# A hybrid decoder trunk on one core: normalisation rows applied through DRAM at the output projection's load

## Chip, cores and metric

The kernel runs on one core of a Trainium2 chip. The metric is the device time of one launch in microseconds; the time of a kernel is the median of its runs.

## What is computed

Two layers over 1024 positions of width 1024, all in float32. Each layer normalises its input, projects it once, and hands the pieces to three mixers that run side by side: a gated linear recurrence (512 channels in four blocks of 128), differential attention (four heads of 128) and a matrix-memory recurrence, "mLSTM" (four heads of 128). Their 1536 outputs go through one output projection; a convolutional gated MLP follows. Every mixer output is normalised by an RMS factor per position, and it is this step that the change touches:

```python
def rmsnorm(x, g):
    y = xf * lax.rsqrt(jnp.mean(xf * xf, axis=-1, keepdims=True) + EPS)
    return (y * g).astype(x.dtype)

y_rg = rmsnorm(gelu(gb) * h, norm_g)                 # over all 512 channels
o    = rmsnorm(o, norm_g) * (1.0 - lambda_init)      # attention, per head of 128
h    = rmsnorm(h, norm_g.reshape(H, dh)) * sigmoid(o_pre)   # mLSTM, per head of 128
x = x + concatenate([y_rg, y_da, y_ml], axis=-1) @ w_out[l]
```

## The kernel before, in words

Activations lie with channels on the 128 partitions and the 1024 positions along the free dimension. So the sum of squares over channels is a sum over partitions, and the factor of a position must come back to all partitions before it can multiply.

Every large product is done three times in a rounded format (`mm3`, L130: high times high, low times high, high times low), after `split` (L126) has cut a tile into its high part (ScalarE) and its low part (VectorE).

A mixer's RMS factors are made in three steps. `compact` (L244) takes the squares of a 128x1024 tile and multiplies them, 128 positions at a time, with a column of ones: eight matmuls with one output column, so that position 128i+p lands in row p and column i of a 128x8 tile. `rsqrt` (L222) turns the small tile into factors with some ten VectorE instructions. `bcast_half` (L235) brings the factors of 512 positions back: four matmuls, each with one column of the factors broadcast as the stationary operand and the identity as the moving one, into a PSUM tile of 128x512.

- `rg` (L467), the recurrence, runs once per block. It writes the unscaled output `u` to DRAM (L502), squares it on ScalarE (L503), compacts the squares (L246) and adds the result to `rgacc`, a 128x8 tile (L507, L509). After the fourth block the factors `rg_r` are made.
- `da_attn` (L634), attention, one head in two halves of queries (`A0` to `A7`). After the second half it squares `o`, compacts, makes the factors, multiplies `o` in place from the two PSUM tiles (L696) and stores it (L698).
- `ml_head` (L819), mLSTM, the same in two halves (`M0` to `M7`), with the scaling at L891 and the store at L894.
- `yload` (L1004) reads four of the twelve stored tiles back (L1009) and splits them into operands of the output projection. For the recurrence (`y0`) the factors are broadcast first, copied by ScalarE into an SBUF tile `rgb` (L996), and each tile is multiplied on load (L1011). For attention (`y1`) and mLSTM (`y2`) nothing is multiplied there.
- `w_out` (L896) multiplies four loaded tiles with four of the eight column blocks of the output weights (`w0` to `w5`), and adds the result to the residual.

The order of all this is a list of steps per layer written out by hand (`ORDER`, L32); `step` (L966) turns a step's name into a call. A scheduler of the framework sets the order on each engine from the program's order, a priority (`high_priority` for a few instructions) and a model of durations; every engine then works through its own queue strictly in order, and so do the DMA queues: SyncE (SP) issues nearly all DMAs, GpSimd (POOL) those that accumulate. A DMA whose tile is not yet free or whose source is not yet written holds back all DMAs behind it on its queue.

Tiles come from small rings, and a new one waits until the oldest is released: `mu` has 2 tiles of 128x1024 (used by the convolutions, the recurrence's operands, the value projection and `rgb`), `p4` 4 (the loaded tiles among others), `o4` 2 (`o`, `num`, the squares), `mr` 3 of 128x512 (the decay rows `R` and `E` of mLSTM), `x16` 2 of four rows each (the recurrence's work space, attention's probabilities, the residual), `h4` 16 (the operands of the projections), and PSUM `aux` 2 banks (compacts, broadcasts, transposes, sums). mLSTM's rows `R` (L851) are DMAs that broadcast one row of DRAM to 128 partitions; POOL masks them (L852) before ScalarE takes their exponential.

Of the kernel before, what the change touches and what calls it, by code (L numbers as in the profile page):

```python
# [32 lines left out]
    "v0 r s0 R0 q0 g q2 q3 q1 A0 z3 z1 v1 A1 z0 A2 R1 z2 A3 A4 A5 M0 M1 z6 A6 A7 z5 z4 z11 M2 z8 R2 M3 R3 z7 z9 z10 y1 M4 y0 M5 w3 M6 s1 w1 M7 w0 w2 y2 w5 w4".split(),  # L33
    "R0 q0 q1 g z0 v0 z7 v1 q3 A0 q2 A1 A2 z2 A3 A4 z1 z3 z5 A5 M0 z4 z6 M1 R1 A6 A7 M2 z8 R2 M3 R3 z11 M4 z9 z10 y1 M5 y0 M6 M7 w3 w2 w0 w1 y2 w4 w5".split(),
# [18 lines left out]
class Trunk:  # L53
# [181 lines left out]
    def bcast_half(self, r, j, ps):  # L235
        nc = self.nc
        pb = ps.tile([P, HALF], F32, tag="aux", name=self.nm("pbc"))
        for i in range(4):
            c = 4 * j + i
            nc.tensor.matmul(pb[:, i * P : (i + 1) * P], r[:, c : c + 1].broadcast_to([P, P]),  # L240
                             self.ident, start=True, stop=True)
        return pb

# [223 lines left out]
    def rg(self, l, n):  # L467
        nc, a, d = self.nc, self.a, self.lay[l]
        if n == 0:
            self.rgacc = self.sm("rgacc", (P, 8), bufs=1)  # L470
        for _ in (0,):
# [32 lines left out]
            pc = self.aux()  # L504
            self.compact(pc, i, self.ones_d)
            if n == 0:
                nc.vector.tensor_copy(self.rgacc, pc[:, :8])  # L507
            else:
                nc.vector.tensor_tensor(self.rgacc, self.rgacc, pc[:, :8], ALU.add)  # L509
        if n < 3:  # L510
            return
        v = self.sm("nv", (P, 8))
        nc.vector.tensor_scalar(v, self.rgacc, 2.0, EPS, ALU.mult, ALU.add)
        self.rg_r = self.sm("rgr", (P, 8), bufs=1)
        self.rsqrt(self.rg_r, v)
# [118 lines left out]
    def da_attn(self, l, h, g):  # L634
# [49 lines left out]
        if g == 0:  # L684
            return
        sq = self.o4("sq")
# [7 lines left out]
        for j in range(2):  # L694
            t = slice(j * HALF, (j + 1) * HALF)
            nc.vector.scalar_tensor_tensor(o[:, t], o[:, t], d["dn2"], self.bcast_half(r, j, self.ps), ALU.mult, ALU.mult)  # L696
        self.yd[4 + h] = self.dr("yd")
        nc.sync.dma_start(self.yd[4 + h], o)  # L698
# [120 lines left out]
    def ml_head(self, l, h, hf):  # L819
# [69 lines left out]
        for j in range(2):  # L889
            t = slice(j * HALF, (j + 1) * HALF)  # L890
            nc.vector.scalar_tensor_tensor(num[:, t], num[:, t], d["mn2"][:, h : h + 1],  # L891
                                           self.bcast_half(r, j, self.ps), ALU.mult, ALU.mult)
# [19 lines left out]
    def mixer(self, l):  # L912
        nc = self.nc
        with ExitStack() as c:
# [4 lines left out]
            self.yd = [None] * 12  # L919
# [46 lines left out]
    def step(self, l, step):  # L966
# [19 lines left out]
        elif k == "z":  # L986
            self.ml_z(l, n // 3, n % 3)
        elif k == "M":
            self.ml_head(l, n // 2, n % 2)
        elif k == "R":  # L990
            self.rg(l, n)
        elif k == "y":
            if n == 0:
                rb = self.mu("rgb")
                for j in range(2):
                    self.nc.scalar.copy(rb[:, j * HALF : (j + 1) * HALF], self.bcast_half(self.rg_r, j, self.ps))  # L996
                self.ys[n] = self.yload(range(4), rb, self.lay[l]["rn"])
            else:
                self.ys[n] = self.yload(range(4 * n, 4 * n + 4))
        elif k == "w":  # L1000
            ms = range(4 * (n % 2), 4 * (n % 2) + 4)
            self.w_out(l, 4 * (n // 2), self.ys[n // 2], self.x[ms[0]] is None, ms)

    def yload(self, ks, rb=None, g=None):  # L1004
        nc = self.nc
        ys = []
        for k in ks:
            st = self.p4("yst")
            nc.sync.dma_start(st, self.yd[k])  # L1009
            if g is not None:  # L1010
                nc.vector.scalar_tensor_tensor(st, st, g[:, k : k + 1], rb, ALU.mult, ALU.mult)  # L1011
            hi, lo = self.h4("yh"), self.h4("yl")
# [318 lines left out]
```

## Time and profile before

| | us |
|---|---|
| median of 3 runs | 2988.64 |
| lowest and highest run | 2980.81, 2997.79 |
| the profiled execution's own time | 3000.99 |
| span of its trace | 2999.3 |
| granted TensorE clock, mean over the span | 0.978 |

The profile is one execution. PE is TensorE's matmuls, PEld its weight loads, DVE VectorE, ACT ScalarE, POOL GpSimd, SP SyncE; a "q" marks a queue's issuing. Matmuls are pipelined, so that the time one costs is the distance between two starts and not its printed duration. A float32 matmul has two records, one in the rounded format has one. The granted clock is a share of full speed (2.4 GHz); 0.5 is the lower level of 1.2 GHz. The first layer's mixers fill about 60 to 770 us of the span, its MLP lasts to about 1505, the second layer's mixers to about 2225.

### The profile page before, as it was taken

The page shows a single profiled execution, that of the slowest core. Times are in us where ns is not written, and L with a number is a line of the kernel's source. Part 1 is how long each engine was busy: PE and PEld are TensorE (multiplying, and loading weights), DVE is VectorE, ACT ScalarE, POOL GpSimd, SP SyncE. Part 2 cuts the span into 40 slices and gives each one's busy share as a digit, 9 for nine tenths or more (in the row PEclk, how much of TensorE's full clock was granted, in tenths as well). Part 3 has the DMA queues.
Part 4 walks back from the last instruction along what each step waited for, and adds up shares of the span by engine and source line. Part 5 has one row for each costly group of instructions (what it writes and reads, how often), then busy time and mean ns, then how long its engine had stood idle before and what let it go on. Part 6 is the DMA issues. An engine that isn't in the chain of part 4 may idle for free.

```text
span 2999.3 us, 37078 instructions
## 1 busy us (share of the span) xinstructions
PE 2898.1 (97%) x13433; PEld 2363.2 (79%) x13433; DVE 2065.0 (69%) x3399; ACT 1346.3 (45%) x2160; POOL 280.5 (9%) x304
## 2 busy tenths in 40 slices
PE   8999999999999999999999999999998999999998
PEld 6777777877878888778877877787776788887887
DVE  5674787786698888844384378787756988887434
ACT  4423655653454444522252346566424544444223
POOL 1000002112111111000010000202111111110000
PEclk9999999998999999999999999999999999999999
DMA  5332224353455555543423322325543555556323
GB/s 188 84 98 95 79 68 123 91 201 112 123 116 127 127 127 127 162 142 95 142 74 102 98 85 92 94 78 161 162 115 99 116 127 123 127 127 211 103 71 110
DMA packets 403428, 352.57 MB, mean 118 GB/s; under 512 B 22226, under 2 KB 348684, under 8 KB 403244
## 3 DMA queue, kind: packets, MB, share of 16 engines
q1 hardware_dynamic: 355900, 326.33, 35.2%
q0 software_dynamic: 46464, 23.07, 6.3%
q8 instruction: 106, 1.74, 0.2%
q10 hardware_dynamic: 880, 0.79, 0.1%
q14 instruction: 78, 0.64, 0.1%
HBM read 263.61 MB, written 86.51 MB: 117 GB/s over the span
## 4 chain that ended last, share of the span: by engine, by line
PE 79%; DVE 8%; DMA 5%; ACT 3%; issue 2%; POOL 1%; SPq 0%; DVEq 0%; POOLq 0%; ACTq 0%
PE z L137 23%; PE z L136 23%; PE z L135 23%; DMA R<-Rd 2%; PE aux L246 2%; DMA fst<-fa 1%; PE pbc L240 1%; PE sc L655 1%; PE sc L656 1%; PE aux L135 1%; PE aux L671 1%; PE aux L136 1%; PE aux L137 1%; DVE wlo L128 1%; POOL ds L864 0%
## 5 line engine op out<-in xcount | busy, mean ns | idle before, releaser
L127 ACT CAST whi<-wraw 128x512 fp32r<-128x512 f32 (+1 forms) x416 | 254.4, 613 | 717.6 <-PE z L136 534.8
L128 DVE TENSOR_TENSOR wlo<-wraw,whi 128x512 fp32r<-128x512 f32 (+1 forms) x416 | 284.3, 684 | 150.1 <-ACT whi L127 146.7
L136 PE MATMUL z<-hl,whi 128*128 128x512 f32 x896 | 363.5, 406 | 4.7 <-DVE hl L265 4.7
L135 PE MATMUL z<-hh,whi 128*128 128x512 f32 x896 | 363.4, 406 | 0.9 <-DVE mpad L459 0.9
L137 PE MATMUL z<-hh,wlo 128*128 128x512 f32 x896 | 362.0, 404 | 0.0
L135 PE MATMUL z<-xh,whi 128*128 128x512 f32 x704 | 276.8, 394 | 5.3 <-ACT cv L1171 2.8
L136 PE MATMUL z<-xh,whi 128*128 128x512 f32 x704 | 276.2, 392 | 4.3 <-DVE xh L128 4.3
L135 PE MATMUL z<-ah,whi 128*128 128x512 f32 x704 | 271.9, 392 | 8.1 <-ACT ah L127 7.8
L137 PE MATMUL z<-xh,wlo 128*128 128x512 f32 x704 | 275.4, 391 | 0.0
L136 PE MATMUL z<-ah,whi 128*128 128x512 f32 x704 | 273.8, 390 | 0.2 <-DVE ah L128 0.2
L137 PE MATMUL z<-ah,wlo 128*128 128x512 f32 x704 | 273.5, 390 | 0.0
L1148 DVE SCALAR_TENSOR_TENSOR fc<-cv,fpar,fc 128x1024 f32<-128x1024 f32 x176 | 222.0, 1281 | 2.9 <-ACT fc L1145 0.6
L127 ACT CAST whi<-fraw 128x512 fp32r<-128x512 f32 x180 | 111.4, 619 | 246.4 <-PE z L136 239.9
L135 PE MATMUL z<-xu,whi 128*128 128x512 f32 x528 | 205.8, 390 | 0.3 <-ACT cv L1171 0.3
L136 PE MATMUL z<-xu,whi 128*128 128x512 f32 x528 | 205.5, 389 | 0.0
L137 PE MATMUL z<-xu,wlo 128*128 128x512 f32 x528 | 205.3, 389 | 0.0
L136 PEld LDWEIGHTS z<-hl,whi 128*128 128x128 f32 x896 | 172.8, 193 | 41.3 <-DVE hl L265 9.0
L135 PEld LDWEIGHTS z<-hh,whi 128*128 128x128 f32 x896 | 173.0, 193 | 34.0 <-DVE mpad L459 0.9
L137 PEld LDWEIGHTS z<-hh,wlo 128*128 128x128 f32 x896 | 173.0, 193 | 31.7
L1140 POOL DMA_DIRECT2D fraw<-in_w_up_dram x88 | 113.3, 1304 | 733.7 <-DVE cv L1171 343.8
L135 PEld LDWEIGHTS z<-ah,whi 128*128 128x128 f32 x704 | 131.5, 188 | 39.6 <-ACT ah L127 12.0
L135 PEld LDWEIGHTS z<-xh,whi 128*128 128x128 f32 x704 | 133.2, 189 | 35.1 <-ACT xh L127 4.1
(384 smaller groups left out, 6134.0 us busy)
## 6 DMA issues: line engine op xcount, KB each, us to landing
wraw<-in_w_up_dram SPq DMA_DIRECT2D x128, 256.0 KB
wraw<-in_w_in_dram SPq DMA_DIRECT2D x112, 256.0 KB
wraw<-in_w_down_dram SPq DMA_DIRECT2D x112, 256.0 KB
fraw<-in_w_up_dram SPq DMA_DIRECT2D x92, 256.0 KB
fraw<-in_w_up_dram POOLq DMA_DIRECT2D x88, 256.0 KB, 5.7
fa<-fc SPq DMA_DIRECT2D x44, 512.0 KB
xd<-x SPq DMA_DIRECT2D x32, 512.0 KB
x<-xd SPq DMA_DIRECT2D x32, 512.0 KB
```

The lines of the kernel that those rows point to most:

```text
L127: self.nc.scalar.copy(hi, src)
L128: self.nc.vector.tensor_tensor(lo, src, hi.bitcast(F32), ALU.subtract)
L135: nc.tensor.matmul(out, ah, bh, start=start and i == 0, stop=False, **kw)
L136: nc.tensor.matmul(out, ah, bl, start=False, stop=False, **kw)
L137: nc.tensor.matmul(out, al, bh, start=False, stop=stop and i == last, **kw)
L240: nc.tensor.matmul(pb[:, i * P : (i + 1) * P], r[:, c : c + 1].broadcast_to([P, P]), self.ident, start=True, stop=True)
L246: self.nc.tensor.matmul(pc[:, i : i + 1], sq[:, i * P : (i + 1) * P], ones, start=True, stop=True)
L655: nc.tensor.matmul(dst, qq[c][:, qs], k[:, :kn], start=True, stop=False)
L656: nc.tensor.matmul(dst, ql[c][:, qs], k[:, :kn], start=False, stop=kb < g)
L671: nc.tensor.transpose(pa[:, k * P : (k + 1) * P], pp[0][:, (4 * kb + k) * P : (4 * kb + k + 1) * P], self.ident)
L1140: nc.gpsimd.dma_start(t, rows(*more), accum_op=ALU.add)
L1148: nc.vector.scalar_tensor_tensor(o, u[:, j : j + S], cw[:, j, col : col + 1], o, ALU.mult, ALU.add)
```

## The change

Seven of a layer's eight head factors (four attention heads, mLSTM heads 0 to 2) and the recurrence's factor are no longer broadcast by matmuls. `row_out` transposes the 128x8 factors to 8x128, copies them out of PSUM and writes them to DRAM as one row of 1024; `row_in` loads such a row into a `mu` tile, broadcast to 128 partitions; `yload` multiplies there. mLSTM head 3 stays as it was. The recurrence's squares are written to a DRAM tile by the first block and added to it by accumulating DMAs of POOL for the other three; a new step `c` loads the sum, compacts it once and makes the factors.

```diff
+    (ORDER, first layer)  ... z7 z9 c z10 y1 M4 y0 ...
+    (ORDER, second layer) ... R3 z11 M4 c z9 z10 y1 M5 y0 ...
...
+    def row_out(self, r):
+        nc = self.nc
+        t = self.dr("rbd", (8, P))
+        pt = self.aux()
+        nc.tensor.transpose(pt[:8, :P], r, self.ident)
+        c = self.tp.tile([P, HALF], F32, tag="mr", bufs=3, name=self.nm("rt"))[:8, :P]
+        nc.scalar.copy(c, pt[:8, :P])
+        nc.sync.dma_start(t, c)
+        return t
+
+    def row_in(self, t, dst):
+        self.nc.sync.dma_start(dst, t.rearrange("i p -> (i p)").unsqueeze(0).broadcast_to([P, S]))
+        return dst
...
     def rg(self, l, n):
...
-            self.rgacc = self.sm("rgacc", (P, 8), bufs=1)
+            self.rgacc = self.dr("rgacc")
...
             nc.scalar.activation(i, u, AF.Square)
-            pc = self.aux()
-            self.compact(pc, i, self.ones_d)
-            if n == 0:
-                nc.vector.tensor_copy(self.rgacc, pc[:, :8])
-            else:
-                nc.vector.tensor_tensor(self.rgacc, self.rgacc, pc[:, :8], ALU.add)
-        if n < 3:
-            return
-        v = self.sm("nv", (P, 8))
-        nc.vector.tensor_scalar(v, self.rgacc, 2.0, EPS, ALU.mult, ALU.add)
-        self.rg_r = self.sm("rgr", (P, 8), bufs=1)
-        self.rsqrt(self.rg_r, v)
+            nc.gpsimd.dma_start(self.rgacc, i, **({"accum_op": ALU.add} if n else {}))
+
+    def rg_stats(self):
+        nc = self.nc
+        t5 = self.p4("rgs")
+        nc.sync.dma_start(t5, self.rgacc)
+        pc = self.aux()
+        self.compact(pc, t5, self.ones_d)
+        v, r = self.sm("nv", (P, 8)), self.sm("nr", (P, 8))
+        nc.vector.tensor_scalar(v, pc[:, :8], 2.0, EPS, ALU.mult, ALU.add)
+        self.rsqrt(r, v)
+        self.rg_r = self.row_out(r)
...
     (da_attn)
+        self.yd[4 + h] = self.dr("yd")
+        nc.sync.dma_start(self.yd[4 + h], o)
         sq = self.o4("sq")
...
         self.rsqrt(r, v)
-        for j in range(2):
-            t = slice(j * HALF, (j + 1) * HALF)
-            nc.vector.scalar_tensor_tensor(o[:, t], o[:, t], d["dn2"], self.bcast_half(r, j, self.ps), ALU.mult, ALU.mult)
-        self.yd[4 + h] = self.dr("yd")
-        nc.sync.dma_start(self.yd[4 + h], o)
+        self.yrow[4 + h] = self.row_out(r), d["dn2"]
...
     (ml_head)
-        for j in range(2):
-            t = slice(j * HALF, (j + 1) * HALF)
-            nc.vector.scalar_tensor_tensor(num[:, t], num[:, t], d["mn2"][:, h : h + 1],
-                                           self.bcast_half(r, j, self.ps), ALU.mult, ALU.mult)
+        if h < 3:
+            self.yrow[8 + h] = self.row_out(r), d["mn2"][:, h : h + 1]
+        else:
+            for j in range(2):
...
         self.yd[8 + h] = self.dr("yd")
         nc.sync.dma_start(self.yd[8 + h], num)
...
     (step)
             if n == 0:
-                rb = self.mu("rgb")
-                for j in range(2):
-                    self.nc.scalar.copy(rb[:, j * HALF : (j + 1) * HALF], self.bcast_half(self.rg_r, j, self.ps))
+                rb = self.row_in(self.rg_r, self.mu("rgb"))
...
+        elif k == "c":
+            self.rg_stats()
...
     (yload)
+            elif k in self.yrow:
+                row, w = self.yrow[k]
+                nc.vector.scalar_tensor_tensor(st, st, w, self.row_in(row, self.mu("yrb")), ALU.mult, ALU.mult)
```

## Rows read from the trace of the kernel before

**Rows 1.** The page: busy time by engine; the chain that ended last, by engine.

```profile
PE 2898.1 (97%) x13433; PEld 2363.2 (79%) x13433; DVE 2065.0 (69%) x3399; ACT 1346.3 (45%) x2160; POOL 280.5 (9%) x304
...
PE 79%; DVE 8%; DMA 5%; ACT 3%; issue 2%; POOL 1%; SPq 0%; DVEq 0%; POOLq 0%; ACTq 0%
```

**Rows 2.** Stretches: us; PE, PEld, DVE, ACT, POOL busy; clock; DMA share; GB/s.

```profile
600.00:635.00 35.00, 34.42 (x172) 28.77 (x171) 26.50 (x49) 19.44 (x21) 0.75 (x2) 0.95 0.61 213
635.00:680.00 45.00, 41.54 (x207) 33.55 (x206) 38.74 (x52) 24.70 (x38) 7.04 (x8) 1.00 0.52 170
```

**Rows 3.** Timeline of PE: start, duration; a broadcast, a compact, five transposes, and what follows.

```profile
609.39 1.95 PE L240 MATMUL pbc<-identr,nr 128*128 128x128 f32 x16
611.09 0.48 PE L137 MATMUL z<-hh,wlo 128*128 128x512 f32 x1
...
603.45 1.84 PE L246 MATMUL aux<-ones_h,sq 128*128 128x1 f32 x16
605.15 0.47 PE L136 MATMUL rgz<-ul,rgw 128*128 128x512 f32 x1
...
335.05 0.71 PE L671 MATMUL aux<-identr,p 128*128 128x128 f32 x5
335.52 0.47 PE L135 MATMUL z<-hh,whi 128*128 128x512 f32 x1
```

**Rows 4.** Groups by line: recurrence's compacts; busy, mean ns, idle before and its releaser.

```profile
L246 PE MATMUL aux<-ones_d,rg 128*128 128x1 f32 x128 | 17.0, 263 | 10.6 <-ACT rg L503 10.6
```

**Rows 5.** Stretches right behind six of the eight recurrence compacts, columns as in rows 2.

```profile
132.00:136.00 4.00, 4.00 (x12) 3.17 (x11) 3.42 (x7) 1.25 (x2) 0.00 (x0) 0.57 0.04 4
...
374.00:382.00 8.00, 8.00 (x32) 6.51 (x32) 3.59 (x8) 1.63 (x4) 0.00 (x0) 0.57 0.02 6
...
589.00:600.00 11.00, 11.00 (x40) 9.65 (x40) 4.90 (x10) 5.05 (x8) 2.12 (x3) 0.53 0.69 179
...
627.00:631.00 4.00, 4.00 (x12) 3.15 (x11) 2.41 (x10) 3.04 (x4) 0.00 (x0) 0.57 0.59 173
...
2053.00:2058.00 5.00, 5.00 (x24) 4.41 (x24) 3.42 (x7) 0.97 (x2) 1.06 (x2) 0.66 0.39 105
...
2088.00:2095.00 7.00, 7.00 (x26) 6.32 (x26) 3.15 (x16) 0.80 (x3) 0.57 (x2) 0.51 0.44 104
```

**Rows 6.** The scalings and small copies: duration min/median/max in ns, first and last start.

```profile
L696 DVE SCALAR_TENSOR_TENSOR o<-o,par,pbc x16: 737/748/750, 332.8 to 2020.3; 128x512 f32<-128x512 f32 x16
...
L1011 DVE SCALAR_TENSOR_TENSOR yst<-yst,par,rgb x8: 1272/1279/1285, 669.6 to 2167.6; 128x1024 f32<-128x1024 f32 x8
...
L871 ACT ACTIVATE mpc<-aux x16: 162/173/176, 471.7 to 2198.9; 128x4 f32<-128x4 f32 x16
```

**Rows 7.** SP's loads of the stored tiles, and ScalarE's splits of them.

```profile
L1009 SPq DMA_DIRECT2D yst<-yd x24: 319/320/596, 600.3 to 2218.7; - x24
L127 ACT CAST yh<-yst x24: 1030/1047/1052, 635.4 to 2222.0; 128x1024 fp32r<-128x1024 f32 x24
```

**Rows 8.** The chain in order of time: broadcast row loads; R3's compact, layer one.

```profile
683.36 3.40 DMA R<-Rd
...
717.34 5.35 DMA R<-Rd
...
624.64 1.95 PE aux L246 x16
```

**Rows 9.** Waits of SP's queue: us in total, times, longest.

```profile
SPq L111 <- DVE wlo L128: 714.8, 214, 16.3
...
SPq L894 <- DVE num L891: 24.4, 8, 6.4
```

**Rows 10.** The page: POOL's accumulating DMAs of the MLP, issue and landing.

```profile
L1140 POOL DMA_DIRECT2D fraw<-in_w_up_dram x88 | 113.3, 1304 | 733.7 <-DVE cv L1171 343.8
...
fraw<-in_w_up_dram POOLq DMA_DIRECT2D x88, 256.0 KB, 5.7
```

**Rows 11.** Matmuls that broadcast the recurrence's factors: duration in ns, first and last start.

```profile
L240 PE MATMUL pbc<-identr,rgr x32: 270/275/276, 666.7 to 2157.5; 128*128 128x128 f32 x32
```

More of the change, by code (lines that the diff above doesn't have):

```diff
@@ L32 @@
 ORDER = (
-    "v0 r s0 R0 q0 g q2 q3 q1 A0 z3 z1 v1 A1 z0 A2 R1 z2 A3 A4 A5 M0 M1 z6 A6 A7 z5 z4 z11 M2 z8 R2 M3 R3 z7 z9 z10 y1 M4 y0 M5 w3 M6 s1 w1 M7 w0 w2 y2 w5 w4".split(),
-    "R0 q0 q1 g z0 v0 z7 v1 q3 A0 q2 A1 A2 z2 A3 A4 z1 z3 z5 A5 M0 z4 z6 M1 R1 A6 A7 M2 z8 R2 M3 R3 z11 M4 z9 z10 y1 M5 y0 M6 M7 w3 w2 w0 w1 y2 w4 w5".split(),
+    "v0 r s0 R0 q0 g q2 q3 q1 A0 z3 z1 v1 A1 z0 A2 R1 z2 A3 A4 A5 M0 M1 z6 A6 A7 z5 z4 z11 M2 z8 R2 M3 R3 z7 z9 c z10 y1 M4 y0 M5 w3 M6 s1 w1 M7 w0 w2 y2 w5 w4".split(),
+    "R0 q0 q1 g z0 v0 z7 v1 q3 A0 q2 A1 A2 z2 A3 A4 z1 z3 z5 A5 M0 z4 z6 M1 R1 A6 A7 M2 z8 R2 M3 R3 z11 M4 c z9 z10 y1 M5 y0 M6 M7 w3 w2 w0 w1 y2 w4 w5".split(),
 )
@@ L888, in ml_head @@
         nc.vector.scalar_tensor_tensor(num, th, 1.0, num, ALU.add, ALU.mult)
-        for j in range(2):
-            t = slice(j * HALF, (j + 1) * HALF)
-            nc.vector.scalar_tensor_tensor(num[:, t], num[:, t], d["mn2"][:, h : h + 1],
-                                           self.bcast_half(r, j, self.ps), ALU.mult, ALU.mult)
+        if h < 3:
+            self.yrow[8 + h] = self.row_out(r), d["mn2"][:, h : h + 1]
+        else:
+            for j in range(2):
+                t = slice(j * HALF, (j + 1) * HALF)
+                nc.vector.scalar_tensor_tensor(num[:, t], num[:, t], d["mn2"][:, h : h + 1],
+                                               self.bcast_half(r, j, self.ps), ALU.mult, ALU.mult)
         self.yd[8 + h] = self.dr("yd")
@@ L918, in mixer @@
             self.tp = self.pool(c, "mt", 2)
-            self.yd = [None] * 12
+            self.yd, self.yrow = [None] * 12, {}
             self.pads = [self.tp.tile([P, S + 3], F32, tag=f"mpad{i}", bufs=1, name=self.nm("mpad"))
```

## The prediction

> **What bounds the kernel now.** I read the busy times and the chain of waits first [rows 1]. TensorE's matmuls are busy for 97% of the span and make up 79% of the chain that ended last; no other engine has more than 8% of it. So an instruction taken off TensorE is worth nearly its own time, unless it stood in a stretch where something else ends last. The stretches tell where that may be [rows 2]: ahead of the output projection TensorE is filled, 34.4 of 35 us; while the operands are loaded and split, VectorE has 38.7 of 45 us and TensorE only 41.5. There VectorE and transfers count too. What an instruction of TensorE costs I take from the distance between starts, since printed durations overlap [rows 3].
>
> **What leaves TensorE.** A row's broadcast is two calls, 16 records, from 609.39 to 611.09: 1.70 us [rows 3]. Per layer four attention heads, three mLSTM heads and the recurrence lose theirs: 16 rows x 1.70 = 27.2 us. A compact is 16 records from 603.45 to 605.15, also 1.70 us [rows 3]. The recurrence has 8 of them (128 records, [rows 4]) and keeps one a layer: 6 x 1.70 = 10.2 us. New are 16 transposes of 128x8. The nearest row is five transposes of 128x128 in 335.05 to 335.52, 0.094 us each [rows 3]: 1.5 us. Net 27.2 + 10.2 - 1.5 = 35.9 us. Since some of this lay beside VectorE's full stretches, I count nine tenths, **-32**; between 24 (only two thirds bound) and 36.
>
> **Waits and clock around the compacts.** TensorE stood idle 10.6 us in all before the eight recurrence compacts, each time for ScalarE's square [rows 4]: its queue is in order, and the compact came round before the squares were there. Six of eight go: 8 us; the remaining two wait for a DMA instead, so I take **-6**, between 0 and -10.6. Behind six of the eight compacts the granted clock fell to the level of 1.2 GHz: over the six stretches, length x (1 - clock) is 1.7 + 3.4 + 5.2 + 1.7 + 1.7 + 3.4 = 17.1 us of lost work [rows 5]. In the worst, TensorE had waited for the square and then done one-column matmuls, and the clock stood at 0.53 for 11 us. That is 2.1 us a compact, 12.8 for six. A wait elsewhere can take the clock down as well, so I take about half, **-7**, between 0 and -17.
>
> **VectorE.** Gone are 14 rows' scalings out of PSUM, 28 x 0.748 = 20.9 us (attention's row; mLSTM's have the same shape); new are 14 scalings at load, each like the one that the recurrence's tiles already have there, 14 x 1.279 = 17.9 us [rows 6]. In sum that is -3, but the work moves, out of the attention and mLSTM steps, where TensorE hides it, into the loads. There VectorE is 76% to 86% busy [rows 2]. The loaded tiles wait for operand space: the first load is issued at 600.3, the first split runs at 635.4 [rows 7], and a scaling needs no such space, so most of them can be done early. I let a third show, **+6**, between 0 and 17.9.
>
> **The rows through DRAM.** Per layer SP gets eight row stores, eight row loads and one load of the summed squares: 34 issues at 0.32 us [rows 7], 11 us on a queue that mostly waits for free weight tiles (714.8 us, [rows 9]); no cost by itself. A row store waits for ScalarE's copy, and weight loads and mLSTM's rows stand behind it. But the old store waited there too, for the scaled tile: 24.4 us in 8 times for mLSTM's [rows 9]. From the factors to the old store lay 1.70 + 2 x 0.75 = 3.2 us; to the new one a transpose and a small copy, near 0.09 + 0.17 us [rows 3, 6]. The queue is released earlier. The unscaled tile's store can go before the factors exist.
>
> A row load brings 4 KB to 128 partitions, 512 KB written. The trace has such broadcasts only of up to half that, landing in 3.4 to 5.35 us [rows 8]; the whole I bound by 3.4 and 10.7 (twice the longer). If all are early, nothing is seen; if all 16 showed in full at 5.5, 88 us. Against that stands the 35 us lead of the loads [rows 7]: before, a tile loaded for `y1` lay ready for that long. Each load takes one of two `mu` tiles, which it holds only until its scaling. I count one load in all as seen, near 4.4, the middle of the two rows: **+4**, between 0 and 88.
> The Trainium skill, "DMA: Bandwidth & Descriptors", section "Anatomy of one DMA — SWDGE (gpsimd) path", speaks against the change: a DMA costs about 2.0 us before its bytes at 436 GB/s, mostly the receipt from the target memory. An estimate from it is 2.0 us for a row's store and 3.2 for its load, 83 us for 16 round trips if none were covered. The trace's 3.4 to 5.35 us for less data says that here a load is dearer than this.
>
> The recurrence's squares: eight DMAs of POOL. Its accumulating DMAs in the MLP take 1.304 us to issue and 5.7 to land for 256 KB [rows 10]; for 512 KB I bound the landing by 5.7 and 11.4. POOL is 9% busy [rows 1], but in the mixers it masks mLSTM's rows, and a DMA that waits for its square holds a mask behind it. 8 x 1.304 = 10.4 us is the upper bound without such a wait; I take **+1**. The slack of `c` in the first layer: the last square is compacted from 624.64 [rows 8], its factors are broadcast at 666.7 [rows 11]. With 1.3 + 11.4 for the accumulate and 5.35 for the load the sum is in SBUF at 643; compact, factors, row store and row load have 24 us more. In the second layer it is longer. What covers it are `z10` and `y1`; without them `w0` would start late.
> ScalarE gets 16 small copies near 0.17 us and loses four copies of `rgb`; at 45% [rows 1] that costs nothing. The recurrence's work space is held until POOL's DMA has read the squares, some 7 us longer; its next users are far behind the projections that fill TensorE, so nothing.
>
> **Sum.** -32 - 6 - 7 + 6 + 4 + 1 = -34. The profiled execution took 3000.99 us, so it would have taken 2967; its time lies 12.4 above the median of the runs, 2988.64, inside the highest, 2997.79. Put on the median: **2954.6**. A change is told from none at about 0.5%, 15 us.
>
> **Rivals.**
> *Covered anyway.* What leaves TensorE lay beside work that ends last in any case: two thirds of 36 is 24, waits and clock give nothing since other waits take their place, VectorE shows 6 to 10: -14 to -18, some 2973. For it: VectorE's full 635 to 680 us [rows 2]. Against it: the broadcasts of attention lie between 330 and 560 us, where TensorE is filled by projections.
> *The clock comes back whole.* All 35.9, 10.6 and 17.1 with no new wait: -64, about 2925. For it: the stretches in rows 5 stand right behind these compacts. Against it: heads' own compacts and sums remain.
> *SP held by row loads; the one that ends slower.* In `y1`, `y0` and `y2` a row load stands at the head of SP's queue until a `mu` tile is free, which needs the previous row to land and be scaled: 3.4 to 5.35 + 1.28, some 5.5 us a load, and the output weights wait behind it. Sixteen such holds are 88 us; they outweigh the 38 us gained without this term once 2.4 us of each show, and end beyond +0.5% (2988.64 + 15) from 3.3 us of each on; in full it would be about 3039. For it: two tiles only, and weight loads that already wait up to 16.3 us for their tiles [rows 9]. Against it: the scheduler places a load where it expects the tile to be free, and the lead of 35 us [rows 7].
> *It hardly changes.* The order of all queues is drawn anew, and unlucky places eat the gain: near 2985.
>
> **How the numbers follow.** Forecast (2935 to 2966) 0.55; clock back whole (2915 to 2935) 0.12; covered anyway (2966 to 2982) 0.20, of which 0.12 lies below 2973.7; hardly changed 0.05; SP held 0.08. So faster 0.79, same 0.13, slower 0.08. The range leaves out the slower rival, half of the unchanged case and the best of the clock's: 2920 to 2984.
>
> **What would show it.** Right: L240 and the recurrence's compacts gone from TensorE's groups, some 350 fewer records of these two lines; no idle time before a compact in the recurrence; higher clock behind 374, 589 and 2088 us; stretches ahead of the loads shorter by the number of broadcasts in them. Wrong: SP's queue waiting at the row loads with TensorE idle at the output projection; POOL's masks late behind an accumulate; VectorE at 90% in the loads with operands late; new stretches at 0.5 of the clock.

## The result, and the profile after

The changed kernel takes 3011.59 us (median of 6 runs, 3008.56 to 3020.43), the kernel before on the same chip 2989.05 (6 runs): a ratio of 1.0069, 95% interval 1.0053 to 1.0085. It is slower by some 20 us, where 34 us of gain were forecast. The profiled execution took 3015.51 us, its span is 3013.7.

The page of the changed kernel, busy time by engine and the chain that ended last, answers to [rows 1]:

```profile
PE 2887.2 (96%) x13097; PEld 2323.7 (77%) x13097; DVE 2063.7 (68%) x3377; ACT 1345.3 (45%) x2171; POOL 288.1 (10%) x312
...
PE 77%; DVE 8%; DMA 6%; issue 4%; ACT 4%; POOL 1%; SPq 0%; DVEq 0%; POOLq 0%; ACTq 0%
```

The removal happened as said: 336 records fewer on PE ("some 350"). But busy time fell by only 10.9 us, and span less busy time, TensorE's idle time, rose from 2999.3 - 2898.1 = 101.2 to 126.5 us. The view of the cores gives the mean granted clock, 0.978 before and 0.974 now, so (1 - clock) x span rose from 66 to 78 us. Busy time less this lost time is a rough measure of TensorE's work at full clock: 2832 before, 2809 after. The table does this sum for the kernels below (the clock has three digits, so each figure is good to some 2 us; and these are single executions, that of rg_only the fastest of its runs).

| kernel | span | PE busy | idle | clock, lost | work at full clock |
|---|---|---|---|---|---|
| before | 2999.3 | 2898.1 | 101.2 | 0.978, 66 | 2832 |
| after | 3013.7 | 2887.2 | 126.5 | 0.974, 78 | 2809 |
| pad64 | 3001.7 | 2878.4 | 123.3 | 0.974, 78 | 2800 |
| heads_only | 3020.1 | 2896.7 | 123.4 | 0.971, 88 | 2809 |
| rg_only | 2968.2 | 2868.2 | 100.0 | 0.984, 47 | 2821 |
| ml_rows | 2980.3 | 2884.4 | 95.9 | 0.981, 57 | 2828 |
| load_both | 3016.6 | 2902.7 | 113.9 | 0.975, 75 | 2827 |
| store_rows | 3018.0 | 2915.0 | 103.0 | 0.976, 72 | 2843 |

Every run's span and clock are on record too. As a mean over all runs of a kernel, lost clock is 80 us in the changed kernel, 81 in heads_only, 76 in load_both, 73 in store_rows and 51 in rg_only; in the kernel before, run beside the experiments, it is 60 to 63 in each set.

Where the idle time lies, the stretches of the changed kernel show (us; PE, PEld, DVE, ACT, POOL busy; clock; DMA share; GB/s), the first two the same as in [rows 2]:

```profile
600.00:635.00 35.00, 20.21 (x86) 15.94 (x84) 24.62 (x43) 12.24 (x15) 0.87 (x1) 0.76 0.58 187
635.00:680.00 45.00, 41.30 (x179) 32.23 (x178) 37.25 (x48) 20.09 (x34) 11.22 (x13) 0.89 0.75 241
2100.00:2140.00 40.00, 28.20 (x93) 21.10 (x94) 27.91 (x41) 15.04 (x24) 10.82 (x9) 0.67 0.68 204
```

From 600 to 635 TensorE is busy for 20.2 us where it was for 34.4, and the clock is at 0.76. The kernel before has 35.66 us of PE and a clock of 0.91 in 2100 to 2140. Around both TensorE first reads operands of the output projection (`y1`, the attention heads). The waits of PE in the changed kernel name them (us in total, times, longest):

```profile
PE z L135 <- ACT yh L127: 15.9, 3, 9.6
PE aux L882 <- POOL ds L876: 12.9, 13, 2.9
...
PE aux L248 <- DVE nr L232: 6.8, 3, 6.3
```

And PE's timeline of the changed kernel shows the first layer's in order:

```profile
619.20 3.54 PE L260 MATMUL aux<-ones_d,rgs 128*128 128x1 f32 x16 [3.72 <-DMA rgs<-rgacc]
...
630.08 0.37 PE L248 MATMUL aux<-identr,nr 128*8 128x128 f32 x1 [6.28 <-DVE nr L232]
...
634.60 0.79 PE L135 MATMUL z<-yh,whi 128*128 128x512 f32 x1 [4.14 <-ACT yh L127]
```

TensorE waits for the sum (the compact of `c`), then for the factors so that it can transpose them, then for the first split operand. The waits stand one behind the other because its queue is in order; in 617 to 639 the clock is 0.53 in the view of stretches, the lower of its two levels, 1.2 GHz, for most of the time. The longest wait for `yh`, 9.6 us, is the second layer's. These are two of the signs that the prediction had named for being wrong: TensorE idle at the output projection, and new stretches near 0.5 of the clock.

Two other rows of the changed kernel matter below: POOL's accumulates (duration of the issue in ns, KB each, us to landing) and SP's waits for the row copies.

```profile
L518 POOL DMA_DIRECT2D rgacc<-rg x8: 630/872/905, 129.8 to 2082.8; - x8
...
rgacc<-rg POOLq DMA_DIRECT2D x8, 512.0 KB, 5.7
...
L250 ACT COPY rt<-aux x16: 238/254/256, 326.9 to 2163.8; 8x128 f32<-8x128 f32 x16
...
SPq L251 <- ACT rt L250: 38.2, 10, 6.5
```

### The profile page after: what moved, and what is told of

The parts are those of the page before. It is cut to its first block, busy times and chain, and to the rows that moved or that the text cites. A ratio compares the mean times of both kernels' runs of the same rounds, so it can differ in the third digit from the quotient of the medians.

```text
span 3013.7 us, 36461 instructions
## 1 busy us (share of the span) xinstructions
PE 2887.2 (96%) x13097; PEld 2323.7 (77%) x13097; DVE 2063.7 (68%) x3377; ACT 1345.3 (45%) x2171; POOL 288.1 (10%) x312
## 4 chain that ended last, share of the span: by engine, by line
PE 77%; DVE 8%; DMA 6%; issue 4%; ACT 4%; POOL 1%; SPq 0%; DVEq 0%; POOLq 0%; ACTq 0%
PE z L136 22%; PE z L137 22%; PE z L135 22%; DMA R<-Rd 2%; DMA fst<-fa 1%; PE sc L669 1%; PE aux L260 1%; PE aux L685 1%; PE sc L670 1%; DVE wlo L128 1%; PE aux L135 1%; PE aux L136 1%; PE aux L137 1%; DVE W L128 1%; POOL ds L876 0%
## 5 line engine op out<-in xcount | busy, mean ns | idle before, releaser
L135 PE MATMUL z<-yh,whi 128*128 128x512 f32 x384 | 154.7, 404 | 15.9 <-ACT yh L127 15.9
```

The source lines that it names most:

```text
L135: nc.tensor.matmul(out, ah, bh, start=start and i == 0, stop=False, **kw)
```

## The experiments

"The small tiles" are `rgacc` and `rgr`, 32 bytes a partition each, which left the small pool with the change. Every ratio is to the kernel before on the same chip, with its 95% interval.

**First: which part loses?** The theory was that the new step `c` costs, since its two waits stand in TensorE's queue in order. pad64 is the change with two unused small tiles put back:

```diff
+            for s in ("pad0", "pad1"):
+                nc.vector.memset(self.sm(s, (P, 8), bufs=1), 0.0)
```

> The changed kernel with two small tiles of 32 bytes a partition allocated again and not used, so that every tile allocated after them lies where it lay in the kernel before. Theory (an operand's place in SBUF sets the pace of the matmuls that read it; the MLP lost some 12 us by the shift of 64 bytes): 3011.6 - 12 = about 3000, the matmuls z<-xu back from 0.700 us per three to 0.680. Rival (the MLP's slower pace has nothing to do with the place): 3011, pace 0.700.

heads_only is the kernel before with the seven heads' rows through DRAM and the recurrence untouched; rg_only is the recurrence's sum, `c` and its row through DRAM (with the two pad tiles), and the heads as before. Of the change's parts the first keeps:

```diff
+        self.yrow[4 + h] = self.row_out(r), d["dn2"]
...
+            elif k in self.yrow:
+                row, w = self.yrow[k]
+                nc.vector.scalar_tensor_tensor(st, st, w, self.row_in(row, self.mu("yrb")), ALU.mult, ALU.mult)
```

and the second:

```diff
+            nc.gpsimd.dma_start(self.rgacc, i, **({"accum_op": ALU.add} if n else {}))
...
+        elif k == "c":
+            self.rg_stats()
...
+                rb = self.row_in(self.rg_r, self.mu("rgb"))
```

> The seven head rows through DRAM, the recurrence as it was before (compacts per block, sum in SBUF, broadcast by matmuls), tiles where they lay before. Theory (what cost the time is the recurrence's part: TensorE and SP held by step c): 14 broadcasts of 1.70 us less their transposes, 22 us gained: 2989 - 22 = about 2967. Rival (the row loads at the output projection hold SP and make operands late): 2985 to 3005, with idle time of TensorE before the first output projection of 4 to 10 us in each layer.

> The recurrence's squares and factors through DRAM with step c, the heads scaled as before, tiles where they lay before. Theory (c stands in line on TensorE and SP): gains 16 us (compacts, broadcasts, waits) and clock up to 13, loses 14 us of idle time in layer one, about 6 to 10 in layer two and 10 or more of clock there: 2985 to 3000. Rival (row loads are the cost): about 2965.

In c_late, `c` stands behind `M4` in the first layer and `M5` in the second (pad tiles in):

```diff
-... z9 c z10 y1 M4 y0 ...
-... M4 c z9 z10 y1 M5 y0 ...
+... z9 z10 y1 M4 c y0 ...
+... M4 z9 z10 y1 M5 c y0 ...
```

> The changed kernel with the tiles where they lay before and step c moved behind y1 and M4 (layer one) or M5 (layer two), just ahead of y0. Theory (c in line is the cost, and far behind the last square it waits for nothing): no idle time before the compact and the transpose of c, 2970 to 2980. Rival (row loads are the cost, or y0 is now late): 2995 to 3005.

Measured:

| kernel | us | ratio |
|---|---|---|
| pad64 | 3003.86 | 1.0027 (1.0012 to 1.0041) |
| heads_only | 3016.08 | 1.0068 (1.0045 to 1.0091) |
| rg_only | 2979.89 | 0.9943 (0.9920 to 0.9966) |
| c_late | 2994.78 | 1.0002 (0.9986 to 1.0018) |

The theory fell. The recurrent part with `c` in line is 17 us faster than before (2994 in that set of runs); the heads' rows alone lose as much as the whole change. In rg_only TensorE does wait at `c` for the loaded sum, but not for long:

```profile
PE aux L260 <- DMA rgs<-rgacc: 5.0, 2, 3.6
```

A later `c` gives some 9 us on top of pad64, with intervals that overlap a little, so its place may matter once the heads' rows are there too.

A loss of another kind turned up: putting back two unused tiles is worth 0.42%, some 12 us. They shift every tile of the mixer's and the MLP's pools by 64 bytes. PE's timeline in the MLP of the kernel before and then of the changed kernel:

```profile
1192.37 0.39 PE L135 MATMUL z<-xu,whi 128*128 128x512 f32 x1
1192.59 0.39 PE L136 MATMUL z<-xu,whi 128*128 128x512 f32 x1
1192.82 0.39 PE L137 MATMUL z<-xu,wlo 128*128 128x512 f32 x1
1193.05 0.39 PE L135 MATMUL z<-xu,whi 128*128 128x512 f32 x1
```

```profile
1190.94 0.39 PE L135 MATMUL z<-xu,whi 128*128 128x512 f32 x1
1191.18 0.39 PE L136 MATMUL z<-xu,whi 128*128 128x512 f32 x1
1191.41 0.39 PE L137 MATMUL z<-xu,wlo 128*128 128x512 f32 x1
1191.64 0.39 PE L135 MATMUL z<-xu,whi 128*128 128x512 f32 x1
```

Three matmuls take 0.68 us from start to start before, 0.70 after. The same instructions with `xu`'s tiles 64 bytes earlier run 3% slower, with nothing waiting. The MLP's operand `xh` has its tiles ahead of the small ones, so they did not move; its three matmuls take 0.680 us before and 0.682 after in the mean. The first layer's MLP, from its first matmul to the next mixer's first, took 672.7 us before, 681.6 after and 672.4 in pad64.

**Second: is it the load?** load_pass is the kernel before with a VectorE pass that changes nothing on the 14 tiles; load_rows, with 14 row loads that nobody reads; pool_rows is heads_only with row stores and loads on POOL's queue, not SP's; rg_plus32 is rg_only with 32 unused bytes ahead of all tiles (a constant tile). The first three:

```diff
+            elif k < 11:
+                nc.vector.scalar_tensor_tensor(st, st, 1.0, st, ALU.mult, ALU.max)
```

```diff
+            elif k < 11:
+                nc.sync.dma_start(self.mu("yrb"), self.a["final_norm"].unsqueeze(0).broadcast_to([P, S]))
```

```diff
-        nc.sync.dma_start(t, c)
+        nc.gpsimd.dma_start(t, c)
...
-        self.nc.sync.dma_start(dst, t.rearrange("i p -> (i p)").unsqueeze(0).broadcast_to([P, S]))
+        self.nc.gpsimd.dma_start(dst, t.rearrange("i p -> (i p)").unsqueeze(0).broadcast_to([P, S]))
```

> The kernel before, with one more VectorE pass over each of the 14 attention and mLSTM tiles (heads 0 to 2) at the load; the pass changes no value, and no row is loaded. Theory A (the scaling at the load is the cost: it stands in line on VectorE between load and split): 2994 + 20 to 30. Theory B (the row's load is the cost): 2994 + 0 to 8.

> The kernel before, with 14 row loads of 1024 numbers broadcast to 128 partitions into mu tiles beside the loads of the attention and mLSTM tiles; nothing reads them. Theory B (the row load is the cost: SP stands at a row load until a mu tile of the convolutions is free, with loads behind it): 2994 + 20 or more. Theory A (the pass on VectorE): 2994 + 0 to 8.

> The heads-only kernel with its row stores and row loads on POOL's queue in place of SP's. If what SP holds behind a row store or row load is the cost: 3016 - 15 or more, near 3000. If it is the wait for the row itself (a mu tile, its landing) or the pass on VectorE: 3010 to 3020.

> The recurrence-only kernel with 32 bytes a partition allocated ahead of everything else, so that all operands lie 32 bytes further. If an operand's place sets the pace of the matmuls that read it: three of the MLP's matmuls change from 0.680 us by more than 1%, up or down, and the time with them (0.01 us on some 3500 groups of three is 35 us). If the place has no say, 2980 as without the shift.

| kernel | us | ratio |
|---|---|---|
| load_pass | 2997.52 | 1.0002 (0.9987 to 1.0017) |
| load_rows | 2998.90 | 1.0007 (0.9989 to 1.0026) |
| pool_rows | 3028.12 | 1.0110 (1.0092 to 1.0129) |
| rg_plus32 | 2983.41 | 0.9957 (0.9943 to 0.9972) |

Neither the pass nor the row loads cost anything by themselves, and with the rows on POOL's queue it gets worse, not better. But pool_rows does not free SP, so it does not decide whether a held SP costs. Of the waits of SP's queue there:

```profile
SPq L863 <- DMA rbd<-rt: 34.2, 8, 6.9
```

L863 loads mLSTM's rows `R`, and it waits for the row stores that read `rt`, the small copies: both use the ring `mr`. rg_plus32 is the same as rg_only, in time and in the pace of `xu` (0.680 us).

heads_only's own trace showed what pass and load do together. First SP's queue in the first layer (`mqk<-mu` is the store that frees a `mu` tile of the last convolutions, `yrb` the row load), then PE:

```profile
642.32 0.33 SPq L793 DMA_DIRECT2D mqk<-mu  x1
...
646.64 0.38 SPq L255 DMA_DIRECT2D yrb<-rbd  x1
...
650.03 0.32 SPq L793 DMA_DIRECT2D mqk<-mu  x1
652.43 0.32 SPq L255 DMA_DIRECT2D yrb<-rbd  x1
```

```profile
653.53 1.22 PE L135 MATMUL z<-yh,whi 128*128 128x512 f32 x2 [3.79 <-ACT yh L127]
```

The row load waits for a `mu` tile that the convolutions of `z9` and `z10` still hold: it is issued at 646.64, 4 us behind the store that frees one (3 us behind it in load_rows and load_both). The first split of `y1` follows at 652, where the kernel before had it at 635.4 [rows 7]. In load_rows the loads came as late (from 645.10 on), but nothing waited for them. In heads_only other row loads waited for the scaling of an earlier row to free its `mu` tile, the hold that the rival of the held SP had described. From the waits of SP's queue:

```profile
SPq L255 <- DVE yst L1029: 18.6, 6, 6.5
```

**Third: load and pass together.** load_both is the kernel before with a pass that reads the row and leaves the tile as it is; in heads_qk the rows of heads_only are loaded into halves in the ring `qk`, idle by then; ml_rows sends the rows of three mLSTM heads alone through DRAM; both_qk is pad64 with `qk` for the head rows.

```diff
+                rb = self.mu("yrb")
+                nc.sync.dma_start(rb, self.a["final_norm"].unsqueeze(0).broadcast_to([P, S]))
+                nc.vector.scalar_tensor_tensor(st, rb, 0.0, st, ALU.mult, ALU.add)
```

```diff
-                nc.vector.scalar_tensor_tensor(st, st, w, self.row_in(row, self.mu("yrb")), ALU.mult, ALU.mult)
+                for j in range(2):
+                    t = slice(j * HALF, (j + 1) * HALF)
+                    rb = self.tp.tile([P, HALF], F32, tag="qk", bufs=10, name=self.nm("yrb"))
...
+                    nc.vector.scalar_tensor_tensor(st[:, t], st[:, t], w, rb, ALU.mult, ALU.mult)
```

> The kernel before, with a row load into a mu tile at each of the 14 head tiles of the output projection's load and a VectorE pass that reads that row and the tile but leaves the tile as it is; no rows are stored, no broadcast is removed. Theory C (a head's operand now waits for its row, the row for one of two mu tiles that the last convolutions still hold, and TensorE runs out of projection work): the y1 operands come as late as in the kernel with the heads' rows alone, and the 17 and 26 us that it lost there appear, less what the missing lead hides: 20 to 45 us slower than before (ratio 1.007 to 1.015). Rival (the cost is in the row stores, or in another drawn order): no slower than the load and the pass each were alone, 0 to 6 us.

> The heads' rows alone, as in heads_only, but the row is loaded in two halves into tiles of the ring qk, which the attention no longer uses at that point, in place of mu. Theory C: the row loads are issued at once behind the tile's own load, the first split of y1 starts near 640 us and the lead of 14 us in each layer stays: 2960 to 2980 us, ratio 0.988 to 0.995. Rival (stores or redrawn order): the loss stays, ratio 1.003 to 1.009.

> The rows of the three mLSTM heads alone through DRAM; the four attention heads are scaled before their store, as in the kernel before. Theory C: y1 reads no rows, and y2's are loaded when no convolution holds a mu tile, so the gain of three of seven heads is kept: about 10 us faster, ratio 0.995 to 0.998. Rival (each row store costs): three sevenths of the heads' loss, about 9 us slower, ratio 1.002 to 1.004.

> The whole change, with the two small tiles put back, and the heads' rows in the ring qk in place of mu. Theory C: the gain of the recurrent part alone (16 us) and of the heads with a free ring (15 to 25 us) add up: 2945 to 2970 us, ratio 0.984 to 0.992. Rival: as the whole change with the small tiles back, ratio 1.000 to 1.004.

| kernel | us | ratio |
|---|---|---|
| load_both | 3018.65 | 1.0081 (1.0060 to 1.0103) |
| heads_qk | 3012.07 | 1.0058 (1.0039 to 1.0076) |
| ml_rows | 2982.37 | 0.9958 (0.9945 to 0.9970) |
| both_qk | 2988.89 | 0.9978 (0.9960 to 0.9995) |

load_both settles the load: two things that cost nothing each cost 24 us when the operand has to wait for both. The first splits of `y1` come later. ScalarE's splits in the second layer of the kernel before, then in the first and the second layer of load_both (first and last start; the first layer before begins at 635.4 [rows 7]):

```profile
L127 ACT CAST yh<-yst x8: 1030/1044/1052, 2112.0 to 2168.9; 128x1024 fp32r<-128x1024 f32 x8
...
L127 ACT CAST yh<-yst x8: 1030/1043/1046, 640.7 to 679.3; 128x1024 fp32r<-128x1024 f32 x8
...
L127 ACT CAST yh<-yst x8: 1028/1049/1051, 2130.2 to 2174.6; 128x1024 fp32r<-128x1024 f32 x8
```

And PE's longest waits in load_both:

```profile
PE aux L246 <- ACT rg L503: 10.7, 7, 3.4
PE z L135 <- ACT yh L127: 10.1, 4, 7.4
```

The kernel before has no `yh` row in this view at all; the 10.7 us of the squares are nearly the 10.6 of [rows 4]. The waits are the smaller part of the 24 us: by the table idle time rose by 13, while lost clock rose by 16 over all runs. ml_rows settles which heads: three mLSTM heads' rows, 6 broadcasts x 1.70 = 10.2 us, gain 13 us, so the loss is the attention's. Their operands are `y1`, the first that are read. heads_qk missed: with a ring for the rows that is free the loss stayed, so a full `mu` is not the whole cause. In its first layer the rows were all issued by 621, and the first split ran at 632.9, as early as before; but the splits behind it were late, and TensorE waits 2.0 us at 644.62 for a low half and 6.8 at 653.35 for the next high half. In its second layer all four tiles' rows were issued from 2116.80 on, behind the store of `z9`'s convolution on SP, and the scaling passes were drawn between the last convolutions on VectorE. both_qk gained half of a per cent on pad64, with intervals that don't overlap.

**Fourth: is it the order?** In heads_early and both_early the load, rows and scaling of the four attention tiles are a step `Y` of their own, ahead of `z9` and `z10`; the splits stay at `y1`. rg_ml is rg_only with the rows of the three mLSTM heads.

```diff
-... z7 z9 z10 y1 M4 ...
-... z11 M4 z9 z10 y1 M5 ...
+... z7 Y z9 z10 y1 M4 ...
+... z11 M4 Y z9 z10 y1 M5 ...
```

> As heads_qk, with the loads, rows and scaling of the four attention tiles as a step of their own, drawn ahead of the last convolutions z9 and z10; the splits stay at y1. If the loss is that the scaling stands behind the rows on SP's queue and behind the last convolutions on VectorE, so that the splits come after the last projection has ended, then the tiles are scaled before it ends and the lead is kept: 2960 to 2983 us, ratio 0.988 to 0.996. Rival (VectorE is the bound of this stage whatever the order, or the row stores of the attention cost): the loss stays, ratio 1.002 to 1.008.

> The whole change with the small tiles back, rows in the ring qk, and the attention tiles scaled ahead of z9 and z10. If the order is the cause: 2945 to 2970 us, ratio 0.983 to 0.992. Rival: as both_qk, ratio 0.995 to 1.000.

> The recurrent part through DRAM and the rows of the three mLSTM heads; the attention heads are scaled before their store, as in the kernel before. If the loss sits in the attention's rows alone, the gains of the recurrent part alone (0.9943) and of the mLSTM rows alone (0.9958) add up: 2960 to 2975 us, ratio 0.988 to 0.993. Rival (the stage where y1 is read takes back whatever lead TensorE brings): 0.993 to 0.997.

| kernel | us | ratio |
|---|---|---|
| heads_early | 3015.66 | 1.0061 (1.0041 to 1.0082) |
| both_early | 2981.93 | 0.9958 (0.9943 to 0.9974) |
| rg_ml | 2975.65 | 0.9936 (0.9916 to 0.9955) |

heads_early missed as well, and its trace says where the wait went. The tiles' instructions in the first layer (ns min/median/max, first and last start), a stretch, and PE's timeline:

```profile
L1035 DVE SCALAR_TENSOR_TENSOR yst<-yst,par,yrb x8: 737/745/752, 618.2 to 632.6; 128x512 f32<-128x512 f32 x8
L127 ACT CAST yh<-yst x8: 1027/1042/1052, 624.3 to 679.5; 128x1024 fp32r<-128x1024 f32 x8
L128 DVE TENSOR_TENSOR yl<-yst,yh x8: 1208/1212/1224, 643.9 to 680.6; 128x1024 fp32r<-128x1024 f32 x8
```

```profile
610.00:640.00 30.00, 21.05 (x99) 16.59 (x97) 28.58 (x49) 17.10 (x21) 2.68 (x3) 0.90 0.93 305
```

```profile
645.21 0.79 PE L136 MATMUL z<-yl,whi 128*128 128x512 f32 x1 [12.77 <-DVE yl L128]
```

The tiles are scaled by 633 and the first high half is cast at 624, but VectorE, 28.6 of 30 us busy with the convolutions and the passes, gets to the first low half at 643.9, and TensorE waits 12.8 us for it. As this trace reads, VectorE ends the stretch once the rows are out of the way, and a TensorE that comes earlier waits longer; no run with less VectorE work there tested it. In the whole change the step `Y` with the `qk` ring does show: both_early is 0.69% faster than pad64, some 21 us, though not clearly faster than both_qk. rg_ml has the lowest median of all, but it and rg_only can't be told apart; the two gains (0.57% and 0.42%) add up to 0.64% only.

**Fifth: the stores.** heads_unscaled is heads_only without the load's row and pass (the heads' normalisation is left out); store_rows is the kernel before with the rows of the seven heads also transposed, copied and stored, read by nobody; before_plus64 is the kernel before with the two unused small tiles of pad64, which move later tiles by 64 bytes the other way.

```diff
-            elif k in self.yrow:
-                row, w = self.yrow[k]
-                nc.vector.scalar_tensor_tensor(st, st, w, self.row_in(row, self.mu("yrb")), ALU.mult, ALU.mult)
```

```diff
+        self.row_out(r)
         for j in range(2):
```

> heads_only without the row loads and the scaling pass at the output projection's load: the rows of the seven heads are stored and never applied, so their normalisation is left out. Theory C (the loss is where the operand waits for its row and pass): the broadcasts' 24 us are gained less the stores' small cost, 2960 to 2980 us, ratio 0.988 to 0.995. Rival (the loss lies in the row stores, or in the attention's own stage that the missing broadcasts redraw): ratio 0.999 or more.

> The kernel before with the rows of the seven heads also transposed, copied and stored, and read by nobody. Theory C: seven transposes, copies and stores per layer cost next to nothing, ratio 0.999 to 1.003. Rival (each store holds SP, the ring mr or the attention's own stage): 15 us or more, ratio 1.005 or more.

> The kernel before with two unused small tiles of 32 bytes a partition, which move all later tiles by 64 bytes, as the two tiles that left moved them the other way; nothing else. If the operands' start decides the pace of the MLP's matmuls: 0.700 us for three in place of 0.680, 8 to 14 us slower, ratio 1.0025 to 1.005. Rival (the pace came from something else in the changed kernel): ratio 0.9985 to 1.0015.

| kernel | us | ratio |
|---|---|---|
| heads_unscaled | 2986.59 | 0.9970 (0.9956 to 0.9984) |
| store_rows | 3015.72 | 1.0061 (1.0046 to 1.0076) |
| before_plus64 | 3002.73 | 1.0020 (1.0006 to 1.0035) |

The rival was right this time: the stores alone, read by nobody, cost 18 us. So the heads' loss has two parts, and each takes back most of what the broadcasts gain. From store_rows to heads_unscaled the broadcasts and the old scalings go: -0.91%, a gain of 27 us. From heads_unscaled to heads_only the load's row and pass come: +0.98%, 29 us, where load_both measured +0.81%. So -27 for the broadcasts, +18 for the stores, +24 for the loads: +15 against 20 measured. (With 29 for the loads the sum closes by itself, since the three kernels are steps from one to the next.)

What in the store costs is only partly known. The row copy `rt` takes one of three buffers of the ring `mr`, and mLSTM's decay rows `R` are fetched into the same ring ahead of their use. SP's loads of `R` and its waits, of the kernel before and of store_rows:

```profile
L851 SPq DMA_DIRECT2D R<-Rd x64: 319/339/1478, 178.8 to 2193.2; - x64
...
SPq L894 <- DVE num L891: 24.4, 8, 6.4
SPq L698 <- DVE o L696: 20.5, 5, 5.8
```

```profile
L862 SPq DMA_DIRECT2D R<-Rd x64: 319/332/1399, 460.4 to 2206.1; - x64
...
SPq L251 <- ACT rt L250: 38.4, 13, 8.7
SPq L907 <- DVE num L904: 11.0, 8, 3.0
SPq L709 <- DVE o L707: 9.1, 6, 2.0
```

Before, the first `R` is loaded at 178.8 us and used some 270 us later; with the stores it is loaded at 460.4, about 6 us ahead of its use. The same holds for every kernel here that sends attention rows to DRAM: first load at 438 to 461 in after, pad64, heads_only, c_late, pool_rows, heads_qk, both_qk, heads_early, both_early and heads_unscaled, at 172 to 179 in all the others, ml_rows and load_both among them. In store_rows PE's waits for `R` rise from 1.8 to 7.9 us:

```profile
PE ms L135 <- DVE R L867: 7.9, 6, 1.8
```

That is 6 of 18 us. By the table, idle time as a whole rose by 2 us only, lost clock by some 6 (11 over all runs), and the rest, some 10 us, is busy time spread over many groups of matmuls in pieces of up to 5 us. SP is also held for longer: 38.4 + 11.0 + 9.1 = 58.5 us at stores, against 44.9 before. That the ring makes `R` wait is seen in pool_rows: no row store stands on SP's queue there, and the first `R` is still loaded at 456.7 only, with SP waiting for the stores that read `rt`. ScalarE is a third suspect: in store_rows it stands idle for 25.8 us in 9 times until the transpose is there that it copies; and each transpose takes one of the two `aux` banks. A kernel with the copy in another tile than `mr`'s (the head's own square tile would do) was not run. The loss of the stores is shown; its split between these and the clock stays open.

before_plus64 confirms half. The kernel is slower by 0.2%, and its interval does not reach 1, but by 6 us, not 8 to 14, and the mean of the start-to-start distances of the three `xu` matmuls adds up to 0.688 us (0.680 before, 0.700 after, 0.680 in pad64, over some 500 of each). So the start of the operand alone does change the pace; how the pace depends on it, three starts don't tell.

## Why the prediction was wrong, point by point

**What leaves TensorE (-32)** held. The work at full clock fell from 2832 to 2800 us in pad64, where tile starts are as before: 32 us, good to some 3, where 35.9 were counted and nine tenths of it forecast. In heads_only it fell by 23, where 14 broadcasts less their transposes are 14 x (1.70 - 0.09) = 22.5.

**Waits and clock around the compacts (-6, -7)**: the clock held, the waits did not, and that with the recurrent part alone. Worked out by the prediction's own terms, rg_only removes 10.2 + 2 x 1.70 = 13.6 us of matmuls, 6 of waits and 7 of clock, 27 in all; it gained 17 by its ratio (31 between the two profiled executions, of which its own is its fastest). The row `PE aux L246 <- ACT rg L503` of [rows 4] is gone from its waits, but idle time as a whole fell by 1 us only (101.2 to 100.0): the waits for the loaded sum and others took their place. Lost clock fell by 8 us over all runs (59.5 to 51.4), near the 7 forecast. In the whole change it rose to 78 instead: "a wait elsewhere can take the clock down as well" is what happened, in the stretches 617 to 639 (clock 0.53) and 2113 to 2135 (0.65).

**VectorE (+6)** was too high where it was tested by itself: load_pass measured 0.0002, within 5 us of nothing. The pass is free as long as the tile need not wait for a row.

**The rows through DRAM (+4)** is the step that failed, in two of its sentences.
"Each load takes one of two `mu` tiles, which it holds only until its scaling" looked at one side of the ring: not who holds the tile before. The last convolutions do, until their stores at 642 and 650 us (heads_only). The lead of 35 us that I set against the round trip belongs to the tile's own load; the row and its pass have no such lead. load_both measures the term at 24 us where 4 were counted; the bound of 88 held it. Which link makes the operands late is open in part: the ring was full in heads_only and load_both, but in heads_qk, with a free ring, the loss stayed, where SP's queue and VectorE were late in place of the ring; in heads_early it was VectorE.
"The queue is released earlier" was wrong in sign and left out what shares a ring with the copy. The waits for stores on SP were 44.9 us in 13 times before; in the changed kernel those for row copies alone are 38.2, with 21 more for `num` beside them. The copy took 0.254 us, not 0.17, which is little; but a head now has two stores on SP's queue, each with a wait of its own, and the copy sits in `mr`, which I never listed. store_rows measures the term at 18 us where it was put at nothing.
The prediction's 2.0 us for a row's store and 3.2 for its load, from the Trainium skill, "DMA: Bandwidth & Descriptors", section "Anatomy of one DMA — SWDGE (gpsimd) path", are an estimate by a rule for DMAs that GpSimd issues. Here SP issues the rows. In heads_only a scaling starts at 651.1, within 4.5 us of its row load's issue at 646.64; no view here gives the landing by itself.

**A term was missing**: that a tile which leaves a pool moves all others. Two tiles of 32 bytes that left cost 12 us (after against pad64).

**POOL (+1)** has nothing against it: an accumulate took 0.872 us to issue (1.304 counted) and landed in 5.7 (median), the lower bound set, and TensorE's waits for POOL's `ds` rose only from 11.0 us to 12.9. The Trainium skill, "DMA: Bandwidth & Descriptors", section "Anatomy of one DMA — SWDGE (gpsimd) path", would have 2.0 us and the bytes at 436 GB/s, for 512 KB an estimate of 3.2 us. The trace has 5.7, so an accumulate is dearer than that rule. The slack of 24 us for `c` did not hold, since it was counted up to the recurrence's scaling, while TensorE stands at `c` as soon as its queue gets there: it waits 5.0 us in 2 times for the loaded sum in rg_only (half of what the compacts' squares cost before), and under the whole change two of the three waits from 619 to 635, 10 us, are for `c`.

**The rivals.** The time came out inside what "SP held by row loads" allows, beyond 3004 us and short of 3039, which had a chance of 0.08. Its mechanism came true in part. It named the right resource, the two `mu` tiles, and the right place, `y1`, but not the first holder: SP's queue waited only 8.0 us in 8 times for a previous row's scaling in the changed kernel (18.6 in 6 in heads_only), its price of 5.5 us for each of 16 loads did not occur, and it said nothing of the stores. "Covered anyway" is what heads_early looks like: VectorE's full stretch, 28.6 of 30 us there, ends last as soon as the rows no longer do. In short, forecast -34 and measured about +20: +20 more for the loads, +18 for the stores, +12 for the shifted tiles make +50 of the 54 that lie between. The loads and the stores were each measured on the kernel before, one without the other, so that the sum is a fit and not a proof that they add.

## What to carry to other kernels

When a value that was made in place is sent by way of memory, ask of each new buffer who holds it before, and who will miss it after: here one ring was full at that moment (`mu`, seen in heads_only and load_both; a free ring alone, in heads_qk, was no cure), and into another mLSTM's rows are prefetched (`mr`, seen in the loads of `R` and in SP's waits of pool_rows; its price was not tested by itself). A wait of TensorE can cost more than its length: in load_both idle time rose by 13 us, lost clock by 16. Work taken off the busiest engine pays only where its next operands come earlier too: the same rows through DRAM gained 13 us for the mLSTM heads, which are read last, and lost for the attention heads, which are read first. Split a change with several parts and run the parts: here one of them alone, the recurrent sum, beats both kernels (2979.89 us), with the mLSTM rows 2975.65.

## What was not expected of the hardware

The start of an operand in a partition changes a matmul's pace with nothing else changed: three 128x512 matmuls on `xu` took 0.680 us at the tiles' old place, 0.700 with them 64 bytes earlier, 0.688 with them 64 bytes later; 32 bytes later (rg_plus32) it was 0.680 again, with no difference in the time. Over a kernel of 3 ms this is worth 6 to 12 us, as much as a good change.

A pass that costs nothing and a load that costs nothing cost 24 us together (load_pass 1.0002, load_rows 1.0007, load_both 1.0081): prices taken one at a time don't add up where an operand waits for both.
